# Reciprocal-root chains moved between engines, two small weight vectors stored once, and a mixing step issued later, in a two-block model kernel

## The chip, the cores and the metric

The kernel runs on one core of one Trainium2 chip. The metric is device microseconds of one execution of the whole program; the time before is the median of 3 runs, 1548.84 us (1548.0 to 1549.24).

## The reference, cut to what matters

Two blocks over x of shape (1, 256, 1024), all in float32. Block 1 is a gated spatial unit, a causal attention with forget gates and a SwiGLU layer; block 2 is a mixer of pooling, mLSTM and attention with normalised heads, a cross attention, and 16 experts that each take 32 tokens.

```python
def rmsnorm(x, g):
    r = lax.rsqrt(jnp.mean(xf * xf, axis=-1, keepdims=True) + EPS)
    return xf * r * g
def spatial_gating(u, v, w_s, b_s, g_v):            # chunks of 128 tokens
    v = layernorm(v, g_v)
    mixed = einsum('gts,bcsgd->bctgd', tril(w_s), vc) + b_s
    return u * mixed
def first_block(x, ...):
    h = rmsnorm(x, mix_pre_g); proj = h @ w_in      # u, v_s, q, k, v_a, g_a, g_b, f
    merged = sigmoid(g_a) * spatial_gating(gelu(u), gelu(v_s), ...) + sigmoid(g_b) * attention
    x = x + rmsnorm(merged @ w_out, mix_post_g)
    x = x + rmsnorm(swiglu(rmsnorm(x, ffn_pre_g), w_gate, w_up, w_down), ffn_post_g)
def head_rmsnorm(a, g):                             # 8 query and 2 key heads of 64, one g of 64 for each kind
    return a * lax.rsqrt(mean(a * a, -1) + EPS) * g
def second_block(x, mem, ...):
    x = x + concat[pool, mlstm, attn(head_rmsnorm(q), head_rmsnorm(k))] @ w_out
    x = x + mem_cross_attn(rmsnorm_2(x), mem, ...)
    x = x + ec_moe(rmsnorm_2(x), router_w, w_gu, w_down)   # 16 experts, 24 MB of weights each
    return rmsnorm_2(x, final_norm_g)
```

## The kernel before, in words

The 256 tokens stand as two tiles t of 128 partitions. Weights come from memory through one queue, SyncE's (SP in the profile), in pieces of 1 MB into three buffers named raw. `split` (L57 to L70) turns each piece into a high part, written by ScalarE (L67, two halves), and a low part, written by VectorE (L68, two halves of 1.2 us each), in four buffers named whl. A matmul of float32 precision is then three matmuls on the parts (`mm3`, L86). Activations are split in the same way after they have been transposed: ScalarE writes xh (L118), VectorE writes xl (L119).

A normalisation of a token tile runs over four engines: ScalarE sums squares (L151), VectorE adds two halves (L153), a chain of nine tiny instructions on a 128x1 column makes 1/sqrt (`rstd`, L121 to L139: three to prepare, then three Newton steps of two), VectorE scales the tile (L172 for `scale`, L209 for `post_norm_c`, L332 in the layer norm), TensorE transposes it (L185). Chains of width 1 go to GpSimd (POOL) unless the caller names VectorE; wider ones are on VectorE. Nine chains run on GpSimd: tile 1 of the first norm, both tiles of the layer norm of v, four at the end of block 1's mixing (post norm and next norm, tiles 0 and 1), and two at the end of the SwiGLU layer (tile 1).

Each engine executes its instructions in one fixed order, which a planner sets at compile time with its own estimates of durations; the program's order counts as priority. `issue_after` (in `queued`, with the lists `self.behind`) adds edges by hand, so that certain weight splits stand behind certain norm steps or ahead of them: at the end of block 1's mixing, for example, `post_norm_c` of tile 1 stands behind the low part of a split, and the next `scale` too.

Block 1's mixing projects v (two pieces of 512 columns, `vs`), normalises it, then projects u in four pieces (`proj_W`, g = 0, 2, 4, 6), and multiplies each with the spatial mixing of v (`mixed(g)`, L341: 8 matmuls, then two VectorE operations). Before, `mixed(g - 2)` comes right after projection g. The SwiGLU layer runs over 11 slices j of 256 hidden columns: gate and up of slice j, then the down product of slice j - 1 (`aH`, `aL` are its activations, L546 to L550).

Block 2's small tables are loaded by DMAs in `block2_mix`, which the planner issues early, between the weights of the SwiGLU layer. `g640` holds the head norms' weights spread to 10 heads of 64 in each partition; its first 8 heads are scaled by 0.125 (L665) and the whole is multiplied into q and k (L917).

The experts (`moe`, from L1063) stream 402 MB through 12 slots of 2 MB, eight loads of w_gu and four of w_down an expert (L1083); several slots lie where earlier stages had their buffers. TensorE works on a slot as it lands.

Of the kernel before, what the change touches and what calls it, by code (L numbers as in the profile page):

```python
# [14 lines left out]
OP = mybir.AluOpType  # L15
# [4 lines left out]
D = 1024  # L20
# [6 lines left out]
class Body:  # L27
# [90 lines left out]
        self.nc.scalar.activation(H, src, AF.Copy)  # L118
        self.at["E"] = self.nc.vector.tensor_tensor(L, src, H.bitcast(F32), OP.subtract).ins  # L119

    def rstd(self, ss, n, scale, tag="rs", eng=None):  # L121

        nc = self.nc
        q = self.small.tile([128, 4, n], F32, name="rstd", tag=tag + str(n), bufs=4 if n == 1 else 2)
        v, h, y, t = (q[:, i, :n] for i in range(4))
        e = eng or (nc.gpsimd if n == 1 else nc.vector)
        e.tensor_scalar(v, ss, scale, EPS, OP.mult, OP.add)
        e.tensor_scalar(y.bitcast(I32), v.bitcast(I32), -0.5, float(0x5F3759DF), OP.mult, OP.add)
        e.tensor_scalar(h, v, -0.5, None, OP.mult)
        for _ in range(3):  # L130
            if n == 1:
                e.tensor_scalar(t, y, y, h, OP.mult, OP.mult)
                self.last = e.tensor_scalar(y, t, 1.5, y, OP.add, OP.mult)
            else:
                nc.vector.tensor_tensor(t, y, y, OP.mult)
                nc.vector.tensor_tensor(t, t, h, OP.mult)
                nc.vector.scalar_tensor_tensor(y, t, 1.5, y, OP.add, OP.mult)
        return y
# [18 lines left out]
    def norm_T(self, x, gname):  # L157

        nc = self.nc
        g = self.gain(gname)  # L160
        H = self.sb(self.xt, [128, 8, 256], "xh", F32R, tag="xh")
        L = self.sb(self.xt, [128, 8, 256], "xl", F32R, tag="xl")

        def factor(t, eng=None):
            h = self.work.tile([128, D], F32, name="hn", tag="work")
            r = self.rstd(self.sumsq([x[:, t, 0:512], x[:, t, 512:D]], h), 1, 1.0 / D, eng=eng)
            self.at["s", t] = self.sq
            return h, r

        def scale(t, h, r):  # L170
            for c in (slice(0, 512), slice(512, D)):
                self.at["h", t] = nc.vector.scalar_tensor_tensor(h[:, c], x[:, t, c], r, g[:, c], OP.mult, OP.mult).ins  # L172
            return h

        def trans(t, h):
            self.trans_HL(H, L, h, t)

        return (H, L), factor, scale, trans
# [7 lines left out]
            self.evac_HL(H[:, 4 * q:4 * q + 4, t * 128:(t + 1) * 128], L[:, 4 * q:4 * q + 4, t * 128:(t + 1) * 128],  # L186
                         p.rearrange("p (k c) -> p k c", k=4))

    def post_norm_a(self, t, halves, eng=None):

        junk = self.work.tile([128, D], F32, name="pj", tag="work")
        ss = self.sumsq(halves, junk)
        self.at["q", t] = self.sq
        return self.rstd(ss, 1, 1.0 / D, "rsp", eng)

    def post_norm_b(self, halves, g):

# [15 lines left out]
    def run(self):  # L213
        tc, nc, a, ctx = self.tc, self.nc, self.a, self.ctx
        self.per = self.open("per", 1)
        self.small = self.open("small", 4)
        self.banks = None
        self.behind, self.at = [], {}
        self.psum_pool(acc=4, sm=4)
        self.xtp = ExitStack()  # L220
        self.xt = self.open("xt", 1, self.xtp, "right")
        self.NR, self.NH = 3, 4
        self.ep = self.open("ep", 1)
        self.big = self.open("big", 1)
        rawst = ExitStack()
        self.rawp = self.open("rawp", 1, rawst)
        st = ExitStack()
        self.work = self.open("work", 3, st)
        self.gains = self.open("gains", 2, st)
        per = self.per  # L230
        x = self.x = self.sb(per, [128, 2, D], "x")
        xr = a["x"][0].rearrange("(t p) d -> p t d", p=128)
        nc.sync.dma_start(x[:, 0, :], xr[:, 0, :])
        xT, factor, scale, trans = self.norm_T(self.x, "mix_pre_g")
        nc.sync.dma_start(x[:, 1, :], xr[:, 1, :])
        first = [self.unit(a["w_in"][0], u, 1024) for u in range(2)]
        self.constants()
        mkv = ExitStack()
        self.mkv = self.open("mkv", 1, mkv, "right")
        memp = ExitStack()  # L240
        self.memp = self.open("memp", 1, memp, "right")
        for t in range(2):
            trans(t, scale(t, *factor(t, None if t else nc.vector)))
        xT, wg = self.block1_mix(xT, first)
        xT = self.block1_ffn(xT, wg)
        xT = self.block2_mix(*xT, memp, st)
        self.cross(xT)
        self.close(rawst, mkv, self.xtp)
        self.moe()
        self.psum_st.close()  # L250
# [38 lines left out]
    def block1_mix(self, xT, first):  # L289
        tc, nc, a = self.tc, self.nc, self.a  # L290
        w_in = a["w_in"][0]
        with ExitStack() as es:
# [21 lines left out]
            for q in range(2):  # L314
                p = self.ps()
# [34 lines left out]
            for g in (0, 2, 4, 6):  # L350
                acc = self.proj_W(xT, w_in, 128 * g)
                nc.scalar.activation(pair(z, g), bank(acc), AF.Gelu_apprx_tanh)
                if g:
                    mixed(g - 2)
            mixed(6)

            wfH = self.sb(m1, [128, 8, 8], "wfH", F32R)
# [175 lines left out]
    def block1_ffn(self, xT, wg0):  # L533
# [4 lines left out]
        with ExitStack() as es:  # L538
# [42 lines left out]
                    down(j, acts[j], ds[j], (t,))  # L581

            tail(0)
            r = self.post_norm_a(0, acc[0:2], nc.vector)
            self.post_norm_c(0, self.post_norm_b(acc[0:2], gp), r)
            h = scale(0, *factor(0, nc.vector))
            tail(1)
            r = self.post_norm_a(1, acc[2:4])
            p = self.at
# [31 lines left out]
    def block2_mix(self, xT, wk, wq, trans1, memp, st):  # L621
        tc, nc, a = self.tc, self.nc, self.a
        wi = a["w_in_2"][0]
        with ExitStack() as es:
# [8 lines left out]
            nc.sync.dma_start(cw, a["mlstm_conv_w_2"][0].rearrange("j (b p) -> (j b) p", p=128))  # L633
            mng = self.sb(m2, [128, 256], "mng")
            nc.sync.dma_start(mng, bcast(a["mlstm_norm_g_2"][0]))
            g640 = self.sb(m2, [128, 10, 64], "g640")
            for h0, n, nm in ((0, 8, "q_norm_g_2"), (8, 2, "k_norm_g_2")):
                g1 = a[nm][0]
                nc.sync.dma_start(g640[:, h0:h0 + n, :],
                                    bass.AP(tensor=g1.tensor, offset=g1.offset, ap=[[0, 128], [0, n], [1, 64]]))  # L640
            rope = self.sb(m2, [128, 2, 2, 64], "rope")
            nc.sync.dma_start(rope, a["rope_c"])
            pw = self.sb(m2, [128, 2, 128], "pw")
# [18 lines left out]
                nc.scalar.activation(qa[:, t, 0:8, :], acc.rearrange("p (h e) -> p h e", h=8), AF.Copy)  # L662
            self.close(st)
            nc.vector.tensor_scalar(mng, mng, 0.5, None, OP.mult)
            nc.vector.tensor_scalar(g640[:, 0:8, :], g640[:, 0:8, :], 0.125, None, OP.mult)  # L665
            ms = ExitStack()
            mw = self.open("m2w", 2, ms, "right")
            wg = mw.tile([128, 8, 16], F32, name="wg", tag="pd", bufs=1)
            nc.sync.dma_start(wg, wi.rearrange("(k p) c -> p k c", p=128)[:, :, 1280:1296])
            wqk = [self.split(self.unit_c(wi, 256 + 128 * b)) for b in (0, 2)]  # L670
            self.psum_pool(acc=2, at=3, po=1, sm=2)
            qT, kT = self.attn2_rope(m2, qa, g640, rope)

            wgH = self.sb(m2, [128, 8, 16], "wgH", F32R)
            wgL = self.sb(m2, [128, 8, 16], "wgL", F32R)
# [37 lines left out]
            self.work = self.open("work2", 2, work2)  # L713
            self.gains = self.open("gains2", 1, work2)
            xT, factor, scale, trans = self.norm_T(self.x, "norm_mem_g_2")
            self.proj_out(a["w_out_2"][0], (yH, yL), lambda t: trans(t, scale(t, *factor(t, nc.vector))), ((2, 3, 0, 1), (4, 5, 6, 7)), ("acc", "sm"))
            p = self.at
            self.behind = [(), (p["h", 0], p["s", 0])]
            self.close(work2)
# [182 lines left out]
                nc.tensor.transpose(py[:, b * 256 + t * 128:b * 256 + t * 128 + 128], hf[:, b * 128:(b + 1) * 128], self.ident)  # L902
        self.evac_HL(yH[:, 2:4, :], yL[:, 2:4, :], py.rearrange("p (b t) -> p b t", b=2))

    def attn2_rope(self, m2, qa, g640, rope):
        nc = self.nc
        qT = self.sb(m2, [128, 4, 256], "qT2")
        kT = self.sb(m2, [128, 256], "kT2")
# [3 lines left out]
        ss = self.small.tile([128, 32], F32, name="ss", tag="st6", bufs=1)  # L912
        nc.vector.tensor_reduce(ss[:, 0:20].rearrange("p (t h) -> p t h", t=2), ro, AX.X, OP.add)
        r = self.rstd(ss[:, 0:20], 20, 1.0 / 64)
        qa2, g2 = qa.rearrange("p t h e -> p (t h) e"), g640[:, None].to_broadcast([128, 2, 10, 64])
        nc.vector.tensor_tensor(qa2, qa2, r[:, :, None].to_broadcast([128, 20, 64]), OP.mult)
        nc.vector.tensor_tensor(qa, qa, g2, OP.mult)  # L917
        for t in range(2):
            av2 = qa[:, t].rearrange("p h (f two) -> p h f two", two=2)
            rv = ro[:, t].rearrange("p h (f two) -> p h f two", two=2)  # L920
# [117 lines left out]
    def route(self, t, cw):  # L1038
# [4 lines left out]
        for q in range(2):  # L1043
# [6 lines left out]
                nc.vector.tensor_copy(xf[:, 0:4], p)  # L1050
            else:
                nc.scalar.activation(xf[:, 4:8], p, AF.Copy)
        self.r4[t] = self.rstd(ss, 1, 1.0 / D, eng=nc.vector)
        self.r4_ins[t] = self.last.ins
        nc.gpsimd.tensor_copy(self.rc[:, t:t + 1], self.r4[t])
        p = self.logits[t] = self.ps("po" if t else "at")
# [242 lines left out]
```

## Time and profile before

| | |
|---|---|
| median of 3 runs | 1548.84 us (1548.0 to 1549.24) |
| the profiled execution, its own time | 1550.03 us |
| its span on the core | 1548.3 us |
| mean granted TensorE clock | 0.884 |
| TensorE busy | 1202.1 us (78%) |
| VectorE / ScalarE / GpSimd busy | 421.3 / 352.3 / 37.4 us |
| read from memory | 501 MB |

The span is cut in two by what is busy: up to about 575 us TensorE is busy nearly all the time, afterwards the DMA engines are. A time of the trace is us from the start of the span. In a timeline row the bracket at the end says how long the engine was idle before the instruction and what ended that idle time.

### The profile page before, as it was taken

The page shows a single profiled execution, that of the slowest core. Times are in us where ns is not written, and L with a number is a line of the kernel's source. Part 1 is how long each engine was busy: PE and PEld are TensorE (multiplying, and loading weights), DVE is VectorE, ACT ScalarE, POOL GpSimd, SP SyncE. Part 2 cuts the span into 40 slices and gives each one's busy share as a digit, 9 for nine tenths or more (in the row PEclk, how much of TensorE's full clock was granted, in tenths as well). Part 3 has the DMA queues.
Part 4 walks back from the last instruction along what each step waited for, and adds up shares of the span by engine and source line. Part 5 has one row for each costly group of instructions (what it writes and reads, how often), then busy time and mean ns, then how long its engine had stood idle before and what let it go on. Part 6 is the DMA issues. An engine that isn't in the chain of part 4 may idle for free.

```text
span 1548.3 us, 17883 instructions
## 1 busy us (share of the span) xinstructions
PE 1202.1 (78%) x7685; PEld 684.1 (44%) x7685; DVE 421.3 (27%) x769; ACT 352.3 (23%) x608; POOL 37.4 (2%) x97
## 2 busy tenths in 40 slices
PE   6999998999989999786666666657666566567675
PEld 5998988899978786321112111112111112111112
DVE  5644655545466765300000000000000000000002
ACT  5455544444445744010000000000000000000002
POOL 1100012000020000000000000000000000000000
PEclk9999999999999999898769878788788788877777
DMA  8754444755543349999999999999999999999996
GB/s 284 227 165 143 138 136 152 257 182 189 190 124 124 110 176 407 369 428 427 427 428 427 426 428 428 427 428 426 428 427 427 427 427 427 428 428 426 427 425 233
DMA packets 110127, 503.26 MB, mean 325 GB/s; under 512 B 11083, under 2 KB 65119, under 8 KB 85984
## 3 DMA queue, kind: packets, MB, share of 16 engines
q1 hardware_dynamic: 110048, 502.12, 81.5%
q8 instruction: 60, 0.98, 0.3%
q14 instruction: 19, 0.16, 0.0%
HBM read 501.05 MB, written 1.05 MB: 324 GB/s over the span
## 4 chain that ended last, share of the span: by engine, by line
DMA 54%; PE 2%; SPq 2%; DVE 1%; ACT 0%; issue 0%; DVEq 0%
DMA eraw<-in_expert_w_gu_dram 36%; DMA eraw<-in_expert_w_down_dram 18%; SPq L1233 2%; PE sm L1153 1%; PE sm L1186 1%; PE sm L1135 0%; PE acc L1200 0%; DVE tk L1108 0%; DVE m L1107 0%; DVE OH L1119 0%; ACT L1173 0%; DVE x L1242 0%; PE sm L1177 0%; DVE ys L1198 0%; DVE es L1174 0%
## 5 line engine op out<-in xcount | busy, mean ns | idle before, releaser
L1153 PE MATMUL sm<-eraw,xs 128*32 128x512 f32 x2048 | 330.5, 755 | 190.2 <-DMA eraw<-in_expert_w_gu_dram 190.2
L1153 PEld LDWEIGHTS sm<-eraw,xs 128*32 128x32 f32 x2048 | 63.3, 124 | 429.7 <-DMA eraw<-in_expert_w_gu_dram 289.5
L1186 PE MATMUL sm<-eraw,aT 128*32 128x512 f32 (+2 forms) x1088 | 169.1, 758 | 81.6 <-DMA eraw<-in_expert_w_down_dram 73.4
L68 DVE TENSOR_TENSOR whl<-raw,whl 128x1024 fp32r<-128x1024 f32 x166 | 198.0, 1220 | 107.7 <-ACT whl L67 107.6
L67 ACT ACTIVATE whl<-raw 128x1024 fp32r<-128x1024 f32 x166 | 168.2, 1052 | 91.5 <-issue 49.7
L1174 DVE SCALAR_TENSOR_TENSOR es<-sm,rsl,es 128x512 f32<-128x512 f32 x16 | 12.0, 751 | 465.7 <-PE sm L1153 462.8
L1186 PEld LDWEIGHTS sm<-eraw,aT 128*32 128x32 f32 x1088 | 34.6, 129 | 198.7 <-DMA eraw<-in_expert_w_down_dram 118.3
L1173 ACT ACTIVATE es<-sm,rsl 128x512 f32<-128x512 f32 x16 | 11.0, 687 | 427.2 <-PE sm L1153 427.2
L86 PE MATMUL acc<-xh,whl 128*128 128x256 f32 x704 | 95.8, 286 | 0.0
L86 PE MATMUL sm<-xh,whl 128*128 128x256 f32 x704 | 91.7, 283 | 0.0
L86 PEld LDWEIGHTS acc<-xh,whl 128*128 128x128 f32 x704 | 88.8, 191 | 0.8
L86 PEld LDWEIGHTS sm<-xh,whl 128*128 128x128 f32 x704 | 88.2, 191 | 0.6
L1198 DVE COPY ys<-sm 128x512 f32<-128x512 f32 (+2 forms) x18 | 11.4, 631 | 235.9 <-PE acc L1200 231.4
L86 PE MATMUL acc<-whl,xh 128*128 128x512 f32 x256 | 70.5, 408 | 0.2
L1200 PE MATMUL acc<-ys,ogT 128*128 128x512 f32 (+2 forms) x136 | 66.3, 611 | 5.2 <-DVE ys L1198 4.3
L1196 ACT ACTIVATE ys<-sm 128x512 f32<-128x512 f32 x16 | 9.6, 597 | 229.9 <-PE sm L1186 229.9
L86 PE MATMUL acc<-whl,aH 128*128 128x512 f32 x176 | 57.9, 403 | 2.4 <-ACT aH L118 2.4
L86 PEld LDWEIGHTS acc<-whl,xh 128*128 128x128 f32 x256 | 48.1, 192 | 11.6 <-ACT xh L118 0.6
L86 PE MATMUL acc<-xl,whl 128*128 128x256 f32 x352 | 51.0, 283 | 0.0
L86 PE MATMUL sm<-xl,whl 128*128 128x256 f32 x352 | 48.9, 281 | 0.0
L1200 PEld LDWEIGHTS acc<-ys,ogT 128*128 128x128 f32 x136 | 23.9, 199 | 51.5 <-issue 21.4
L86 PEld LDWEIGHTS acc<-xl,whl 128*128 128x128 f32 x352 | 45.5, 189 | 0.4
(366 smaller groups left out, 1124.0 us busy)
## 6 DMA issues: line engine op xcount, KB each, us to landing
eraw<-in_expert_w_gu_dram SPq DMA_DIRECT2D x128, 2048.0 KB, 39.1
eraw<-in_expert_w_down_dram SPq DMA_DIRECT2D x60, 2048.0 KB, 39.1
raw<-in_w_in_dram SPq DMA_DIRECT2D x34, 1024.0 KB, 5.4
raw<-in_w_gate_dram SPq DMA_DIRECT2D x11, 1024.0 KB, 5.3
raw<-in_w_up_dram SPq DMA_DIRECT2D x11, 1024.0 KB, 5.5
raw<-in_w_down_dram SPq DMA_DIRECT2D x11, 1024.0 KB, 5.0
raw<-in_w_out_dram SPq DMA_DIRECT2D x8, 1024.0 KB, 5.6
eraw<-in_expert_w_down_dram SPq DMA_DIRECT2D x7, 1024.0 KB, 27.8
```

The source lines that it names most:

```text
L67: nc.scalar.activation(H[:, k], raw[:, k], AF.Copy)
L68: self.at["L"] = nc.vector.tensor_tensor(L[:, k], raw[:, k], H[:, k].bitcast(F32), OP.subtract).ins
L86: nc.tensor.matmul(out, l[i], r[j], start=first and p == 0 and q == 0, stop=last and p == 2 and q == n - 1)
L1153: nc.tensor.matmul(dst[32 * j:32 * j + 32, :], xs[:, k, 32 * q:32 * q + 32], raw[:, o + 512 * j:o + 512 * j + 512], start=k == 0, stop=k = ...
L1173: nc.scalar.activation(s, G, AF.Silu, scale=rs)
L1174: nc.vector.scalar_tensor_tensor(s, U, rs, s, OP.mult, OP.mult)
L1186: nc.tensor.matmul(y[c0][32 * c:32 * c + 32, 0:n], aT[:, c, 32 * j:32 * j + 32], raw[:, o:o + n], start=j == 0, stop=j == 3, tile_position ...
L1196: nc.scalar.activation(ys, y[c0][:, 0:n], AF.Copy)
L1198: nc.vector.tensor_copy(ys, y[c0][:, 0:n])
L1200: nc.tensor.matmul(out[t], ogT[:, t * 128:(t + 1) * 128], ys, start=first, stop=last)
L1233: nc.sync.dma_start(raws[j].rearrange("p (i n) -> p i n", i=4)[:, :, c0:c0 + m], rows(j)[:, :, c0:c0 + m])
```

## The change

All chains of `rstd` go to VectorE, whatever their width; the parameter `eng` goes. The two head norms' weights are loaded once per partition, as `gqk` of 128 x 2 x 64, and multiplied in by two VectorE operations with a broadcast operand, one over the 8 query heads and one over the 2 key heads, in place of one over 10. `mixed(g)` comes two projections after projection g, in place of one; the last two come after the last projection.

```diff
-    def rstd(self, ss, n, scale, tag="rs", eng=None):
+    def rstd(self, ss, n, scale, tag="rs"):
...
-        e = eng or (nc.gpsimd if n == 1 else nc.vector)
+        e = nc.vector
...
             for g in (0, 2, 4, 6):
                 acc = self.proj_W(xT, w_in, 128 * g)
                 nc.scalar.activation(pair(z, g), bank(acc), AF.Gelu_apprx_tanh)
-                if g:
-                    mixed(g - 2)
+                if g >= 4:
+                    mixed(g - 4)
+            mixed(4)
             mixed(6)
...
-            g640 = self.sb(m2, [128, 10, 64], "g640")
-            for h0, n, nm in ((0, 8, "q_norm_g_2"), (8, 2, "k_norm_g_2")):
-                g1 = a[nm][0]
-                nc.sync.dma_start(g640[:, h0:h0 + n, :],
-                                    bass.AP(tensor=g1.tensor, offset=g1.offset, ap=[[0, 128], [0, n], [1, 64]]))
+            gqk = self.sb(m2, [128, 2, 64], "gqk")
+            for i, nm in enumerate(("q_norm_g_2", "k_norm_g_2")):
+                nc.sync.dma_start(gqk[:, i, :], bcast(a[nm][0]))
...
-            nc.vector.tensor_scalar(g640[:, 0:8, :], g640[:, 0:8, :], 0.125, None, OP.mult)
+            nc.vector.tensor_scalar(gqk[:, 0, :], gqk[:, 0, :], 0.125, None, OP.mult)
...
-        nc.vector.tensor_tensor(qa, qa, g2, OP.mult)
+        for i, hh in enumerate((slice(0, 8), slice(8, 10))):
+            nc.vector.tensor_tensor(qa[:, :, hh], qa[:, :, hh],
+                                    gqk[:, None, i:i + 1, :].to_broadcast([128, 2, hh.stop - hh.start, 64]), OP.mult)
```

The other lines of the diff drop the argument `eng` from `factor`, `post_norm_a` and their callers.

## Rows read from the trace of the kernel before

**Rows 1.** The page's part 2, 40 slices of the span: busy tenths of the DMA engines.

```profile
DMA  8754444755543349999999999999999999999996
```

**Rows 2.** The chain of work that ended last: start us, us, what.

```profile
673.90 30.19 DMA eraw<-in_expert_w_down_dram
```

**Rows 3.** Timeline of SyncE's queue: start us, us, line, out<-in, count.

```profile
573.58 27.72 SPq L1083 DMA_DIRECT2D eraw<-in_expert_w_gu_dram  x8
```

**Rows 4.** Timeline of a chain of nine on VectorE: its first instruction and its successor.

```profile
441.55 0.15 DVE L127 TENSOR_SCALAR rstd<-ss 128x1 f32<-128x1 f32 x1
443.67 1.42 DVE L172 SCALAR_TENSOR_TENSOR hn<-x,rstd,gain 128x512 f32<-128x512 f32 x2
```

**Rows 5.** Timeline around the first spatial mixing, TensorE and VectorE.

```profile
42.76 2.04 PE L86 MATMUL acc<-xh,whl 128*128 128x256 f32 x16
50.86 0.81 DVE L332 TENSOR_SCALAR vs<-vs,mv,rstd 128x1024 f32<-128x1024 f32 x1 [3.07 <-POOL rstd L133]
53.99 0.94 PE L341 MATMUL sm<-wb,vs 128*128 128x128 f32 x6 [2.41 <-DVE vs L333]
54.69 3.61 PE L86 MATMUL acc<-xh,whl 128*128 128x256 f32 x16
```

**Rows 6.** Timeline of SyncE's queue and VectorE around the load of the query norm's weights.

```profile
254.04 0.43 SPq L639 DMA_DIRECT2D g<-in_q_norm_g_dram  x1
258.53 9.66 SPq L56 DMA_DIRECT2D raw<-in_w_up_dram  x1
272.41 0.43 DVE L665 TENSOR_SCALAR g<-g 128x512 f32<-128x512 f32 x1 [13.70 <-DMA g<-in_q_norm_g_dram]
275.49 1.06 ACT L67 ACTIVATE whl<-raw 128x1024 fp32r<-128x1024 f32 x1 [15.23 <-DMA raw<-in_w_gate_dram]
```

**Rows 7.** Windows: stretch, us, busy of PE PEld DVE ACT POOL, PEclk, DMA share, GB/s.

```profile
260.00:262.00 2.00, 2.00 (x19) 2.00 (x19) 0.00 (x0) 0.25 (x1) 0.00 (x0) 1.00 0.07 20
274.70:286.17 11.47, 8.51 (x24) 6.46 (x25) 9.80 (x11) 7.65 (x9) 0.00 (x0) 0.70 0.91 287
297.56:303.20 5.64, 5.64 (x28) 4.67 (x27) 3.65 (x4) 2.53 (x3) 0.00 (x0) 1.00 0.65 191
```

**Rows 8.** DMA issues: out<-in, queue, count, KB each, median us to landing.

```profile
mng<-in_mlstm_norm_g_dram SPq DMA_DIRECT2D x1, 128.0 KB, 4.7
g<-in_k_norm_g_dram SPq DMA_DIRECT2D x1, 64.0 KB, 6.7
```

**Rows 9.** Timeline at the end of block 1's mixing, VectorE and ScalarE, then TensorE.

```profile
233.88 1.42 DVE L172 SCALAR_TENSOR_TENSOR hn<-x,rstd,gain 128x512 f32<-128x512 f32 x2 [2.15 <-POOL rstd L133]
241.06 1.41 DVE L209 SCALAR_TENSOR_TENSOR x<-pn,rstd,x 128x512 f32<-128x512 f32 x2 [2.23 <-POOL rstd L133]
243.60 1.22 DVE L68 TENSOR_TENSOR whl<-raw,whl 128x1024 fp32r<-128x1024 f32 x1
244.72 3.90 ACT L67 ACTIVATE whl<-raw 128x1024 fp32r<-128x1024 f32 x4
247.88 1.41 DVE L172 SCALAR_TENSOR_TENSOR hn<-x,rstd,gain 128x512 f32<-128x512 f32 x2 [3.06 <-POOL rstd L133]
...
248.78 0.63 PE L185 MATMUL sm<-ident,hn 128*128 128x128 f32 x4 [3.46 <-DVE hn L172]
```

**Rows 10.** VectorE's busy time in a stretch at the end of the SwiGLU layer.

```profile
443.00:448.00 5.00, 4.89 (x11) 1.00 0.00 0
```

**Rows 11.** Timeline behind that stretch, VectorE and TensorE.

```profile
450.35 1.42 DVE L209 SCALAR_TENSOR_TENSOR x<-pn,rstd,x 128x512 f32<-128x512 f32 x2 [0.53 <-POOL rstd L133]
459.43 1.41 DVE L172 SCALAR_TENSOR_TENSOR hn<-x,rstd,gain 128x512 f32<-128x512 f32 x2 [3.06 <-POOL rstd L133]
460.33 1.71 PE L185 MATMUL sm<-ident,hn 128*128 128x128 f32 x8 [2.64 <-DVE hn L172]
```

**Rows 12.** Timeline of VectorE at the start, and in the head norm.

```profile
13.51 1.42 DVE L172 SCALAR_TENSOR_TENSOR hn<-x,rstd,gain 128x512 f32<-128x512 f32 x2 [2.23 <-POOL rstd L133]
...
481.77 1.49 DVE L917 TENSOR_TENSOR qa<-qa,g 128x1280 f32<-128x1280 f32 x1
```

More of the change, by code (lines that the diff above doesn't have):

```diff
@@ L162, in norm_T, with factor @@
         L = self.sb(self.xt, [128, 8, 256], "xl", F32R, tag="xl")
-        def factor(t, eng=None):
+        def factor(t):
             h = self.work.tile([128, D], F32, name="hn", tag="work")
-            r = self.rstd(self.sumsq([x[:, t, 0:512], x[:, t, 512:D]], h), 1, 1.0 / D, eng=eng)
+            r = self.rstd(self.sumsq([x[:, t, 0:512], x[:, t, 512:D]], h), 1, 1.0 / D)
             self.at["s", t] = self.sq
@@ L187, in trans_HL, with post_norm_a @@
                          p.rearrange("p (k c) -> p k c", k=4))
-    def post_norm_a(self, t, halves, eng=None):
+    def post_norm_a(self, t, halves):
         junk = self.work.tile([128, D], F32, name="pj", tag="work")
@@ L193, in post_norm_a @@
         self.at["q", t] = self.sq
-        return self.rstd(ss, 1, 1.0 / D, "rsp", eng)
+        return self.rstd(ss, 1, 1.0 / D, "rsp")
     def post_norm_b(self, halves, g):
@@ L242, in run @@
         for t in range(2):
-            trans(t, scale(t, *factor(t, None if t else nc.vector)))
+            trans(t, scale(t, *factor(t)))
         xT, wg = self.block1_mix(xT, first)
@@ L583, in block1_ffn @@
             tail(0)
-            r = self.post_norm_a(0, acc[0:2], nc.vector)
+            r = self.post_norm_a(0, acc[0:2])
             self.post_norm_c(0, self.post_norm_b(acc[0:2], gp), r)
-            h = scale(0, *factor(0, nc.vector))
+            h = scale(0, *factor(0))
             tail(1)
@@ L671, in block2_mix @@
             self.psum_pool(acc=2, at=3, po=1, sm=2)
-            qT, kT = self.attn2_rope(m2, qa, g640, rope)
+            qT, kT = self.attn2_rope(m2, qa, gqk, rope)
             wgH = self.sb(m2, [128, 8, 16], "wgH", F32R)
@@ L715, in block2_mix @@
             xT, factor, scale, trans = self.norm_T(self.x, "norm_mem_g_2")
-            self.proj_out(a["w_out_2"][0], (yH, yL), lambda t: trans(t, scale(t, *factor(t, nc.vector))), ((2, 3, 0, 1), (4, 5, 6, 7)), ("acc", "sm"))
+            self.proj_out(a["w_out_2"][0], (yH, yL), lambda t: trans(t, scale(t, *factor(t))), ((2, 3, 0, 1), (4, 5, 6, 7)), ("acc", "sm"))
             p = self.at
@@ L903, in mlstm, with attn2_rope @@
         self.evac_HL(yH[:, 2:4, :], yL[:, 2:4, :], py.rearrange("p (b t) -> p b t", b=2))
-    def attn2_rope(self, m2, qa, g640, rope):
+    def attn2_rope(self, m2, qa, gqk, rope):
         nc = self.nc
@@ L914, in attn2_rope @@
         r = self.rstd(ss[:, 0:20], 20, 1.0 / 64)
-        qa2, g2 = qa.rearrange("p t h e -> p (t h) e"), g640[:, None].to_broadcast([128, 2, 10, 64])
+        qa2 = qa.rearrange("p t h e -> p (t h) e")
         nc.vector.tensor_tensor(qa2, qa2, r[:, :, None].to_broadcast([128, 20, 64]), OP.mult)
-        nc.vector.tensor_tensor(qa, qa, g2, OP.mult)
+        for i, hh in enumerate((slice(0, 8), slice(8, 10))):
+            nc.vector.tensor_tensor(qa[:, :, hh], qa[:, :, hh],
+                                    gqk[:, None, i:i + 1, :].to_broadcast([128, 2, hh.stop - hh.start, 64]), OP.mult)
         for t in range(2):
@@ L1052, in route @@
                 nc.scalar.activation(xf[:, 4:8], p, AF.Copy)
-        self.r4[t] = self.rstd(ss, 1, 1.0 / D, eng=nc.vector)
+        self.r4[t] = self.rstd(ss, 1, 1.0 / D)
         self.r4_ins[t] = self.last.ins
```

## The prediction

> **What bounds the kernel now.** First the page's slices: the DMA engines are full from the 16th of 40 slices to the end [rows 1]. Then the chain of waits, read from its end: between 673.90 us and the last loads it holds nearly nothing but loads of expert weights, the first of them in [rows 2]; compute after them and a few hundredths of issue are all the rest. So the end is set by when that stream begins and by its bytes, which the change leaves alone. SyncE's timeline shows the beginning: the first expert load is issued at 573.58 us, into buffers that the stages before have to give up [rows 3]. Up to there TensorE is busy nearly all the time, so I read its timeline for every idle stretch and every slow one ahead of 573 us. What is taken out of these comes off the stream's start and, one for one, off the end; VectorE, ScalarE or GpSimd time as such is worth nothing. Four places matter, and all have a part of the change at their root.
>
> **The price of a chain.** On VectorE the nine instructions run from 441.55 to 443.67, 2.12 us [rows 4]. Nine chains move: 9 x 2.12 = 19.1 us more VectorE work. While a chain runs on GpSimd, VectorE mostly stands idle until it ends, so each move is a difference: 2.12 us of work for an idle time that stands in a bracket.
>
> **Place A, spatial mixing (54 us).** The first mixing's last six matmuls stand 2.41 us idle, waiting for VectorE's gain on v, which itself waited 3.07 us for a GpSimd chain [rows 5]. The idle stretch has a second price: the next 16 projection matmuls take 3.61 us, where the same 16 took 2.04 before, a clock lower for 1.57 us. Now the third projection comes first. It is 48 matmuls at 2.04/16, 6.1 us; put in at about 51.6 (2.41 ahead of 53.99) it has TensorE busy until about 57.5, while the operands are there at 53.99 even with the chains left on GpSimd, and some us earlier with 2.12 in place of 3.07 for each tile. The cover is 3.5 us thick. The mixing's own matmuls are moved, not added; its VectorE steps lie later, but z is not read before the gates, far behind. On SyncE, loads that wait for v's gain go sooner. Sum: -2.41 - 1.57 = -4.0 us; if the cover failed, 0.
>
> **Place B, the query norm's weights (254 to 286 us).** The load issued at 254.04 has 128 x 8 rows of 256 bytes. Everything behind it suffers: SyncE's next-but-one issue takes 9.66 us, VectorE stands 13.70 us in front of its scaling at 272.41 with work behind it in the line, ScalarE waits 15.23 us for a gate weight [rows 6]. Six us after the issue the 16 DMA engines are 0.07 busy and move 20 GB/s [rows 7]: one engine's share, for 256 KB at that rate 13 us. At last TensorE pays: the down product's 24 matmuls of slice 0 fill 11.47 us at clock 0.70; the next slice's take 5.64 with a few more besides [rows 7]. That is 5.83 us of waiting and clock. The new load has 128 rows. Not in the trace, but between 1.6 us (32 KB at 20 GB/s) and the 6.7 that 256 rows took, near the 4.7 of another load of 128 rows [rows 8]; I take 4.7. Landed by 259 to 261, it leaves VectorE over 10 us before the first activation of the layer needs it, so even the upper end costs nothing. -5.8 us; bounds -6.0 and, should the queue stay blocked for another reason, 0. The key weights' second load shrinks too; nobody waits for it.
>
> **Place C, end of block 1's mixing (245 us).** TensorE waits 3.46 us for the scaled tile 1 [rows 9]. Its line goes back through three GpSimd waits. (1) VectorE idles 2.15 us before 233.88 for tile 0's chain; that chain, sooner and shorter, frees VectorE when tile 1's sums arrive: about 1.9 us. (2) The 2.23 us before 241.06 turn into 2.12 us of chain, with the split ahead of it as now: 0.1. (3) From 243.60 to 247.88 there are 4.28 us: half a split, 1.22, and 3.06 of waiting. On VectorE it is 2.12 if the half split goes behind, 3.34 if it stays ahead: 0.9 to 2.2. The tile is 2.9 to 4.2 us sooner. What is late next: ScalarE's four split halves, 3.90 us at 244.72, stand ahead of the evacuation of these very transposes; they move up with ScalarE's sums, by about 2 to 2.5 us. I take -3.2, between the two; bounds -5.0 (ScalarE reordered, some clock back) and -2.0.
>
> **Place D, end of the SwiGLU layer (445 to 460 us).** Here the move costs. VectorE is 4.89 of 5 us busy [rows 10], with splits that the next tile's scaling stands behind by an edge. It waits for GpSimd only 0.53 us before 450.35 and 3.06 before 459.43 [rows 11]. In exchange come two chains: 2 x 2.12 - 0.53 - 3.06 = +0.65 for the scaled tile 1 that TensorE waits for at 460.33. The first chain also precedes tile 0's low part, up to 2.12 for TensorE some us earlier; but TensorE loses 2.64 idle us at 460.33 anyway, and a stall ahead of that is taken out of it. I take +0.6; bounds -0.7 (the shorter last wait leaves the clock up: the eight transposes took 1.71 us at a lower one) and +4.2 (both chains in the open).
> A page speaks against the move exactly here: the Trainium skill, Perfetto Trace Analysis, section "Optimizing Scalar/DVE Operations", says that from a saturated VectorE work may be moved off, even to GpSimd. By it D would cost up to the 4.2; by the rows 0.65, because VectorE was idle waiting for the engine that relieved it. The same section doubts that shifting between these two helps, since they share a port; the 3.06 us wait behind splits agrees in direction.
>
> **Small parts.** At the start VectorE idles 2.23 us for tile 1's chain [rows 12] and would work 2.12 instead: 0; bounds -0.5 and +2.1 (chain put ahead of tile 0's scaling). The product with the norm weights, 1.49 us for 1280 elements [rows 12], becomes one of 1024 and one of 256: the same elements and one more fixed part, +0.1; bounds 0 and +0.4, TensorE having gate projections meanwhile. The scaling by 0.125 shrinks eightfold, in a place where VectorE has room.
>
> **Sum.** -4.0 - 3.2 + 0.6 - 5.8 + 0.1 = -12.3 us. The profiled execution took 1550.03, so 1537.7; the median of the runs is 1.2 lower, so 1536.5. Bounds summed naively: -4.0 - 5.0 - 0.7 - 6.0 - 0.5 = -16.2, so 1532.6; if the planner also reorders block 2 by a us or two in my favour, 1531.
>
> **Rivals.** *VectorE gives part of it back.* At C and D the chains run into splits, D costs 4.2 and C yields 2.0: -4.0 - 2.0 + 4.2 - 5.8 + 0.1 = -7.5, so 1541.3. For it: [rows 10] and the splits' edges. Against it: the brackets, which show that VectorE was idle for the same time. The page's rule named at D would give this outcome, 1541.3. In the same band lies B failing (1542.3): if many reads of one 256-byte row were slow by themselves rather than by their number; the key weights' 256 rows in 6.7 us speak against that.
> *All goes together.* C yields 5.0 and D gains 0.7: -4.0 - 5.0 - 0.7 - 5.8 + 0.1 = -15.4, so 1533.4, and down to 1531 with the other lower bounds.
> *The gain is hidden.* The stream does not start sooner, because something other than TensorE's line gives up its buffers: within 3 us of before, 1548. Against it: the queue's loads ahead of that one belong to stages that TensorE paces, and its slots lie where those stages work.
> *Slower: an in-order VectorE.* Every chain instruction stands in one line with the splits and low parts that TensorE eats. If the planner lays the chains' first instructions, which wait for ScalarE's sums, ahead of ready splits, chains end up on TensorE's line in full: 2.12 each, and where TensorE then stands over 2 us, some 1.6 of clock as in [rows 5], 3.7 together. The moves of mixing and weights bring 4.0 + 5.8 = 9.8, so from the third such chain on nothing is left, and six (all but the layer norm's two and the first) cost 22: 1548.8 - 9.8 + 22 = 1561. Against it: the chain that already stands between a ready tile and TensorE ran unbroken [rows 4].
>
> **Chances.** The forecast (1533.5 to 1540.5) 0.60; part given back, or B failing (1540.5 to 1545.5) 0.16; all together (below 1533.5) 0.10; hidden 0.06; slower 0.08. No change is what lies within 0.2%, 3.1 us, about what a measurement can tell. So faster 0.86, same 0.06, slower 0.08. For the range I keep the forecast, half of "all together" and most of the given-back band up to 1543.5: 1531.5 to 1543.5, about 0.8.
>
> **What would show it.** GpSimd has no 128x1 arithmetic left. A: no TensorE wait for v, the clock whole at 55 to 60. B: no VectorE wait for the query weights above 2 us, the first down product near 5.6 us. C: the wait of 3.46 below 1.5. D: tile 1's transposes 0 to 1 us later against the layer's end than before. The first expert load near 561, and from it to the end the same 975 us within 2. The prediction is wrong if that load moves by less than 8 us, if a new TensorE wait for a VectorE split appears, or if the stretch from the load to the end grows.

## Result and the profile after

The changed kernel takes 1537.2 us (median of 4 runs, 1536.8 to 1539.4), beside 1549.04 for the kernel before on the same chip (4 runs, 1548.0 to 1550.9): ratio 0.9928, 95% interval 0.9912 to 0.9943. The forecast was 1536.5, in a range from 1531.5 to 1543.5. The profiled execution has a span of 1535.2 us, 13.1 less than before; the first expert load is issued 12.58 us sooner, and from it to the end there are 974.2 us (974.7 before). As forecast, the end moved with the start of that stream and, but for 0.5 us, with nothing else; in the traces of all fourteen kernels here that stretch is 973.3 to 975.5 us. On the page GpSimd is down to 5.0 us in 16 instructions and VectorE up to 434.3 from 421.3.

The four places, first on TensorE's timeline (start us, us, engine, line, operation, out<-in, shapes, count, and in brackets the idle time before and what ended it). Line numbers of this kernel differ from the one before by at most one.

```profile
10.77 1.94 PE L185 MATMUL sm<-ident,hn 128*128 128x128 f32 x8 [10.77 <-DVE hn L172]
12.54 2.17 PE L86 MATMUL acc<-whl,xh 128*128 128x512 f32 x4
...
55.19 1.05 PE L341 MATMUL sm<-wb,vs 128*128 128x128 f32 x8
56.00 2.15 PE L86 MATMUL acc<-xh,whl 128*128 128x256 f32 x16
...
243.40 1.93 PE L185 MATMUL sm<-ident,hn 128*128 128x128 f32 x8 [3.88 <-DVE hn L172]
246.09 3.99 PE L86 MATMUL sm<-xh,whl 128*128 128x256 f32 x17 [0.75 <-ACT xh L118]
...
444.81 1.67 PE L86 MATMUL acc<-whl,xh 128*128 128x512 f32 x6 [0.48 <-DVE rstd L127]
...
449.70 1.29 PE L185 MATMUL sm<-ident,hn 128*128 128x128 f32 x8 [1.35 <-DVE hn L172]
```

At 55.19 the wait of 2.41 us of [rows 5] is gone and the clock is whole. At 243.40 the wait of [rows 9] is not shorter but longer, 3.88 for 3.46, with slow matmuls behind it. At 449.70 tile 1's wait of 2.64 [rows 11] is 1.35. The wait of 0.48 at 444.81 is new: it ends 0.06 us after a split half of VectorE (443.53 to 444.75), with the chain instruction behind that half named as what ended it. A new wait for a split is what the prediction had named as a sign of being wrong; here it is small. Of the prediction's other signs, C's (the wait of 3.46 below 1.5) failed.

Now the query norm's weights and the stream, on SyncE's queue, and two windows, the first gate product and the first down product (us, busy of PE, PEld, DVE, ACT, POOL, PEclk, DMA share, GB/s):

```profile
245.62 0.42 SPq L639 DMA_DIRECT2D gqk<-in_q_norm_g_dram  x1
...
251.44 0.38 SPq L56 DMA_DIRECT2D raw<-in_w_up_dram  x1
...
561.00 28.32 SPq L1084 DMA_DIRECT2D eraw<-in_expert_w_gu_dram  x8
```

```profile
246.00:250.00 4.00, 3.91 (x18) 3.91 (x19) 4.00 (x5) 2.76 (x4) 0.00 (x0) 0.50 0.62 208
...
270.58:276.07 5.49, 5.49 (x26) 4.51 (x25) 3.65 (x4) 2.53 (x3) 0.00 (x0) 1.00 0.65 190
```

The issue that took 9.66 us [rows 6] takes 0.38, and the down product that took 11.47 [rows 7] takes 5.49. The gate product behind the longer wait runs at a granted clock of 0.50, the lower of the two levels, 1.2 GHz.

To keep books I use the lead: how much sooner than in the kernel before TensorE starts the same instruction. What the lead gains between two points was gained there. The points are the first u-projection (39.94 us before), the forget gate's first matmul (70.23), the memory keys' second projection (239.37), gate projection 1 (263.14), tile 0's transposes at the end of the SwiGLU layer (444.57), block 2's gate weights (474.23) and the first expert load (573.58). "Start" is the lead at the first point; A is what was gained from the first to the second, C from the third to the fourth, B from the fourth to the fifth, D from the fifth to the sixth. One profiled execution each, us; the last row is the changed kernel's forecast:

| kernel | start | A | C | B | D | lead at load | time, ratio to before |
|---|---|---|---|---|---|---|---|
| changed | 1.65 | 4.20 | -1.97 | 6.38 | 1.72 | 12.58 | 1537.2, 0.9928 |
| mixing alone | -0.13 | 4.09 | -0.50 | 0.30 | -0.27 | 3.45 | 1545.0, 0.9983 |
| weights alone | -0.80 | 1.66 | 0.05 | 6.18 | 0.90 | 8.21 | 1541.6, 0.9965 |
| chains alone | 1.51 | 3.68 | -2.02 | 6.27 | 1.72 | 11.38 | 1538.0, 0.9944 |
| forecast | 0 | 4.0 | 3.2 | 5.8 | -0.6 | 12.3 | 1536.5 |

### The profile page after: what moved, and what is told of

It is laid out like the page before. It is cut to its first block, busy times and chain, and to the rows that moved or that the text cites. A ratio compares the mean times of both kernels' runs of the same rounds, so it can differ in the third digit from the quotient of the medians.

```text
span 1535.2 us, 17874 instructions
## 1 busy us (share of the span) xinstructions
PE 1190.9 (78%) x7685; PEld 677.8 (44%) x7685; DVE 434.3 (28%) x851; ACT 351.7 (23%) x608; POOL 5.0 (0%) x16
## 4 chain that ended last, share of the span: by engine, by line
DMA 54%; PE 2%; SPq 2%; DVE 1%; issue 0%; ACT 0%; DVEq 0%
DMA eraw<-in_expert_w_gu_dram 36%; DMA eraw<-in_expert_w_down_dram 18%; SPq L1234 2%; PE sm L1154 1%; PE sm L1187 1%; PE sm L1136 0%; DVE tk L1109 0%; DVE m L1108 0%; PE acc L1201 0%; DVE OH L1120 0%; DVE x L1243 0%; ACT L1174 0%; PE sm L1178 0%; DVE es L1175 0%; DVE eraw L1251 0%
## 5 line engine op out<-in xcount | busy, mean ns | idle before, releaser
L1154 PE MATMUL sm<-eraw,xs 128*32 128x512 f32 x2048 | 324.3, 742 | 190.2 <-DMA eraw<-in_expert_w_gu_dram 190.2
L68 DVE TENSOR_TENSOR whl<-raw,whl 128x1024 fp32r<-128x1024 f32 x166 | 198.8, 1221 | 116.9 <-ACT whl L67 116.7
```

The lines of the kernel that those rows point to most:

```text
L68: self.at["L"] = nc.vector.tensor_tensor(L[:, k], raw[:, k], H[:, k].bitcast(F32), OP.subtract).ins
L1154: nc.tensor.matmul(dst[32 * j:32 * j + 32, :], xs[:, k, 32 * q:32 * q + 32], raw[:, o + 512 * j:o + 512 * j + 512], start=k == 0, stop=k = ...
```

## Experiments

Times of the runs below are medians, each set against the kernel before on the same chip (1547.5 to 1548.6 there); brackets hold the 95% interval of the ratio to it.

**1 to 3. Each part alone.** Edits: the hunks of the diff for the mixing, for the weights, and for the chains (in the third, one line):

```
-        e = eng or (nc.gpsimd if n == 1 else nc.vector)
+        e = nc.vector
```

> The kernel before with one edit: each spatial mixing stands two projections later; chains and head-norm weights as before. Theory (the parts add up, each acts at its own place): TensorE's wait of 2.41 us for v and the clock lost behind it go, 4.0 to 4.2 us; first expert load near 569.5, time 1544.6 to 1545.2. Rival (the gain at A in the changed kernel needed the layer norm's chains on VectorE too): with v only ready at 53.99 less wait is saved, 2 us or under, 1547. Rival (given back at a later place, as the loads that follow come no sooner): under 1 us, 1548 to 1549.

> The kernel before with one edit: the two head norms' weights are loaded once per partition and spread over the heads in the product; chains and mixing as before. Theory: the slow down product of slice 0 (11.47 us) takes 5.5, lead +6.0 at the start of gate projection 2, and +0.0 at the start of gate projection 1; time 1542.6 to 1543.2. Rival for the loss at the end of block 1's mixing (the load queue's new order costs it, not the chains): gate projection 1 starts 1.5 to 2 us later than its lead before that place, time 1544.5 to 1545.

> The kernel before with one edit: all nine-instruction chains on VectorE; mixing and weights as before. Theory (the chains gain where VectorE idled for them and lose where split halves stand between their instructions): start -1.6, spatial mixing 0 (TensorE still stands some 2.5 us in front of the first mixing), end of block 1's mixing +2.0, end of the SwiGLU layer -1.8, block 2 -0.6: 1546.5 to 1547.5. Forecast's own terms (0, none of A, -3.2, +0.6, 0): 1546.4, but with the end of block 1's mixing 3.2 shorter. Rival (chains cost nothing anywhere, the loss at block 1's mixing comes from the load queue): 1544.5 to 1545.

Measured: mixing 1545.0 (ratio 0.9973 to 0.9992), weights 1541.6 (0.9952 to 0.9977), chains 1538.0 (0.9927 to 0.9961). The first came out as expected, the second 1.0 below its range. The third was a miss by 8.5 us or more, and it overturns the picture of separate places: 2.9 + 6.3 + 9.9 = 19.1 us for the parts, some 12 for the whole. The table shows where: the chains alone bring A's 3.7 and B's 6.3 too, with the mixing where it was and the slow load as it was. At A, the operands of the first mixing come so soon, and the order puts twelve of a projection's 48 matmuls in front:

```profile
49.97 1.65 PE L86 MATMUL acc<-xh,whl 128*128 128x256 f32 x12
51.74 0.93 PE L341 MATMUL sm<-wb,vs 128*128 128x128 f32 x6
```

The run of the weights alone says something else of A. It has the wait of [rows 5] (2.34), yet the 16 matmuls behind it take 2.12 us, not 3.61:

```profile
54.73 0.94 PE L341 MATMUL sm<-wb,vs 128*128 128x128 f32 x6 [2.34 <-DVE vs L333]
55.42 2.12 PE L86 MATMUL acc<-xh,whl 128*128 128x256 f32 x16
```

**4 and 5. Is B hidden by the chains, and by which?** Run 4 is the changed kernel with the weights' hunk undone. Run 5 is chains alone with the four chains of block 1's end left on GpSimd (`post_norm_a(t, acc, nc.gpsimd)` and `factor(t, nc.gpsimd)` in `block1_mix`).

> The changed kernel without its weights edit: chains on VectorE and the later mixing, but the query norm's weights loaded as before, 128 x 8 rows. Theory after the chains alone gave 9.9 us (the parts overlap: with the chains on VectorE the slow load is issued 8 us sooner and lands before TensorE needs what stands behind it): first down product near 5.5 us long, no TensorE wait in front of it, 1536.6 to 1538.0, within 0.7 of the changed kernel. Rival (the forecast's sum, each part at its own place): the 5.8 us come back, 1542 to 1543.5.

> The kernel before with the chains on VectorE except the four at the end of block 1's mixing, which stay on GpSimd; mixing and weights as before. Theory (the gate split's low halves that stand between that chain's instructions free a raw buffer early, SyncE's queue goes on, and the query norm's slow load is issued 8 us sooner; so the loss at block 1's mixing and the hidden load have one cause): without them w_down's first slice and the slow load are issued about as late against TensorE as before, TensorE waits 1.5 to 3 us in front of the first down product and runs it at a lower clock, and 3 to 6 of the 9.9 us are lost: 1541 to 1544. Rival (the chains hide the slow load in some other way): no wait there, and the 1.2 us lost at block 1's mixing are gained, 1536 to 1537.

Measured: 1538.3 (0.9921 to 0.9946; B 6.43) and 1541.9 (0.9950 to 0.9977; C +0.15, B 0.92). Run 5 is as the theory had it, run 4 too, 0.3 above its range. With the chains on VectorE the small load is worth nothing that can be measured; with block 1's four chains back on GpSimd the price returns. SyncE's queue, chains alone first, then run 5:

```profile
241.88 0.37 SPq L556 DMA_DIRECT2D raw<-in_w_down_dram  x1
...
245.99 0.42 SPq L639 DMA_DIRECT2D g<-in_q_norm_g_dram  x1
250.67 0.38 SPq L56 DMA_DIRECT2D raw<-in_w_gate_dram  x1
```

```profile
247.74 0.38 SPq L556 DMA_DIRECT2D raw<-in_w_down_dram  x1
...
249.00 0.43 SPq L639 DMA_DIRECT2D g<-in_q_norm_g_dram  x1
251.21 0.38 SPq L56 DMA_DIRECT2D raw<-in_w_gate_dram  x1
```

Down's first slice waits for a raw buffer. Where a gate unit's low halves run early (next experiment), it is free 5.9 us sooner, and the slow load 3.0 sooner, with TensorE only 0.3 further on. ScalarE still stands 11.25 us for the gate unit behind it, until 268.11, but TensorE comes to the down product at 271.13, without a wait (chains alone, ScalarE and TensorE):

```profile
268.11 1.06 ACT L67 ACTIVATE whl<-raw 128x1024 fp32r<-128x1024 f32 x1 [11.25 <-DMA raw<-in_w_gate_dram]
271.13 0.39 PE L86 MATMUL acc<-whl,aH 128*128 128x512 f32 x1
```

**6. What costs C?** VectorE, and one row of ScalarE, in the changed kernel:

```profile
236.15 0.16 DVE L153 TENSOR_TENSOR ss<-ss 128x1 f32<-128x1 f32 x1
236.22 1.22 DVE L68 TENSOR_TENSOR whl<-raw,whl 128x1024 fp32r<-128x1024 f32 x1
237.36 0.15 DVE L127 TENSOR_SCALAR rstd<-ss 128x1 f32<-128x1 f32 x1
237.42 1.21 DVE L68 TENSOR_TENSOR whl<-raw,whl 128x1024 fp32r<-128x1024 f32 x1
...
239.00 1.22 DVE L68 TENSOR_TENSOR whl<-raw,whl 128x1024 fp32r<-128x1024 f32 x1
240.14 0.21 DVE L133 TENSOR_SCALAR rstd<-rstd 128x1 f32<-128x1 f32 x1
240.26 1.22 DVE L68 TENSOR_TENSOR whl<-raw,whl 128x1024 fp32r<-128x1024 f32 x1
...
242.50 1.42 DVE L172 SCALAR_TENSOR_TENSOR hn<-x,rstd,gain 128x512 f32<-128x512 f32 x2
```

```profile
244.50 1.06 ACT L67 ACTIVATE whl<-raw 128x1024 fp32r<-128x1024 f32 x1 [4.11 <-DMA raw<-in_w_up_dram]
```

The order puts four halves of weight splits in, one between the addition of the sums (L153) and the chain, three inside the chain: addition and chain, 2.31 us without a break (run 7), take from 236.15 to 242.50. Run 6 puts these four chains back on GpSimd in the changed kernel (the edit of run 5).

> The changed kernel with one edit: the four chains at the end of block 1's mixing are on GpSimd as before; everything else as changed. Theory (the 2.0 us lost there come from split halves standing between the chain's instructions on VectorE, which makes 2.12 us of chain last 6.1): the lead over the kernel before, 5.8 at the memory keys' second projection, is 5.8 again at gate projection 1 instead of 3.8, so 2.0 off the changed kernel's 1537.2: 1535.0 to 1535.6. Rival (the gate weights' loads set that place, since ScalarE stands 4.11 us for w_up's first slice ahead of the evacuation): the lead stays 3.8 and the time 1537.

Measured: 1536.05 (0.9916 to 0.9945), C -0.19 for -1.97. The place answers as expected; the total is 0.45 above the expected range and does not separate from the changed kernel's.

**7 and 8. The chain unbroken, with the small load and with the slow one.** Edges make the split halves follow the chain (`queued` orders an instruction behind the named ones of its engine):

```
+        self.at["EA"] = self.nc.scalar.activation(H, src, AF.Copy).ins
...
-            self.behind = [(p["x", 1], p["q", 1])]
+            self.behind = [(p["h", 1], p["q", 1])]
...
-            self.behind = [(p["E"], p["s", 1])]
+            self.behind = [(p["E"], p["s", 1]), (p["E"],), (p["E"], p["EA"])]
```

> The changed kernel with four order edges at the end of block 1's mixing: the low halves of the first gate unit's split stand behind tile 1's scaling on VectorE, those of the next gate unit behind tile 1's low parts, and the next up unit's behind these and, on ScalarE, behind the evacuation of tile 1's transposes. Nothing stands between the chain's instructions then. Theory (broken chain and ScalarE's 4.11 us in front of a weight slice cost the place): chain about 2.1 us, TensorE's wait of 3.88 falls below 1, the 17 gate matmuls take 2.1 to 3.2 instead of 3.99; lead at gate projection 1 from 3.8 to 7 to 8.5; time 1532.5 to 1534.5 where the changed kernel has 1537.2. Rival (the raw buffers come free later, so the next units land later and TensorE waits for them instead): 1536.5 or more, with a new wait for a split.

> The changed kernel with the four order edges of the version that ran at 1530.35, but with the query norm's weights loaded as before, 128 x 8 rows. Theory (the weights edit is worth what the order leaves of the slow load's price): the slow load is issued near 248.6 and lands near 267, TensorE reaches the first down product near 264 and waits 3 us or more for it, then runs at a lower clock: 1535 to 1538, 5 to 7 more than with the small load, although the same edit was worth under 1 in the changed kernel. Rival (the order edges hide the load as the broken chain did): 1530 to 1531.5.

Measured: 1530.35 (0.9870 to 0.9897) and 1530.88 (0.9872 to 0.9905). The first is the fastest kernel here, 6.9 below the changed one (ratio 0.9884 for 0.9928), and beat its expectation: C +4.92, B 6.29, lead at the load 19.16. VectorE, then TensorE, in run 7:

```profile
236.37 0.16 DVE L153 TENSOR_TENSOR ss<-ss 128x1 f32<-128x1 f32 x1
...
238.68 1.42 DVE L172 SCALAR_TENSOR_TENSOR hn<-x,rstd,gain 128x512 f32<-128x512 f32 x2
240.01 2.35 DVE L68 TENSOR_TENSOR whl<-raw,whl 128x1024 fp32r<-128x1024 f32 x2
```

```profile
239.59 1.28 PE L185 MATMUL sm<-ident,hn 128*128 128x128 f32 x8
241.15 2.29 PE L86 MATMUL sm<-xh,whl 128*128 128x256 f32 x17 [0.28 <-ACT xh L118]
```

Addition and chain take 2.3 us, TensorE does not wait for the scaled tile, and the 17 matmuls take 2.29 for 3.99. The split that stood ahead of ScalarE's evacuation is out of the way as well, here as in run 6, so what each of the two cost by itself is not shown. Run 8 went against my theory: B is 6.30 with the slow load too. Its queue and ScalarE show why:

```profile
248.30 0.38 SPq L56 DMA_DIRECT2D raw<-in_w_gate_dram  x1
248.73 0.58 SPq L640 DMA_DIRECT2D g<-in_q_norm_g_dram  x1
252.67 1.33 SPq L56 DMA_DIRECT2D raw<-in_w_up_dram  x1
```

```profile
256.67 1.06 ACT L67 ACTIVATE whl<-raw 128x1024 fp32r<-128x1024 f32 x1 [2.48 <-DMA raw<-in_w_gate_dram]
257.63 0.62 ACT L118 ACTIVATE aH<-si 128x512 fp32r<-128x512 f32 x1
...
270.54 2.01 ACT L67 ACTIVATE whl<-raw 128x1024 fp32r<-128x1024 f32 x2 [10.85 <-DMA raw<-in_w_up_dram]
```

Here the gate unit is issued ahead of the slow load and is there 8.4 us later; the up unit behind it takes 17.9, but the first activation's evacuation (aH) stands ahead of it in ScalarE's line.

**9 and 10. What is the price of the slow load?** Run 9 fetches the same rows by ten loads, run 10 takes VectorE's wait of 13.70 us off the line and leaves the load:

```
+                for h1 in range(h0, h0 + n):
+                    nc.sync.dma_start(g640[:, h1, :], bcast(g1))
```

```
+            with self.queued([self.at["E"]]):
                 nc.vector.tensor_scalar(g640[:, 0:8, :], g640[:, 0:8, :], 0.125, None, OP.mult)
```

> The kernel before with one edit: the same 1280 rows of 256 bytes of head-norm weights are fetched by ten loads of 128 rows instead of one of 1024 and one of 256. Theory (the form of the one load, with its inner stride of 0, is slow): each lands within 4 to 7 us of its issue, VectorE waits under 3 us for them, and the 6 us come as with the smaller load, less up to 1 for eight more issues of 0.43 us on SyncE's queue: 1541.5 to 1543. Rival (the number of reads of one row sets the pace, 20 GB/s in all): the last of the eight lands 13 us or more after the first is issued, and the time is 1546 to 1549.

> The kernel before with one edge: the scaling of the query norm's weights by 0.125, in front of which VectorE stood 13.70 us with the splits and the first activation's product behind it, is ordered behind the last low part of the next layer's transposes, some 190 us later; the load itself stays as it is, 128 x 8 rows. Theory, after the last run (what TensorE pays is the gate unit issued 2 us behind the slow load, which lands only when the slow load is done, some 19 us after its issue, and in front of whose split ScalarE stands with the evacuation for the first down product behind it): VectorE's wait is gone, but ScalarE's 15.23 us for the gate weight, TensorE's 2.42 us and the slow down product stay: 1547 to 1549. Rival (the forecast's wording: VectorE's wait holds up the down product): the first down product takes near 5.5 us without a wait, 1541.5 to 1543.

Measured: 1542.8 (0.9955 to 0.9979; B 6.29) and 1547.96 (0.9987 to 1.0013; B -0.05). So one load of 1024 rows holds up what is behind it, and eight of 128 rows, spread among the weights' loads, do not: the gate unit behind the first of them lands 6.2 us after its issue, for 19.1 before. Two expected numbers were missed: the eight loads land in 8.0 us (median; I had expected 4 to 7), and VectorE stands 6.65 us for the key norm's, though TensorE does not pay for it. Whether the load's form makes it slow or only the number of rows in one load stays open, since what the rival expected came too: the last of the eight lands more than 13 us after the first is issued (254.34; the last is issued near 270). The Trainium skill, DMA: Bandwidth & Descriptors, section "Why a DMA increments its semaphore by 16 and not by 1", would have a load of 128 partitions split over 16 engines; the share of 0.07 in [rows 7] for the one with an inner stride of 0, about one engine's worth of 16, does not agree, and the measurement decides (no row shows which engines worked). Run 10 names the payer. VectorE is free early, and TensorE waits as before, for ScalarE, which stands in front of the gate unit issued 2.2 us behind the slow load:

```profile
263.23 0.69 DVE L547 TENSOR_TENSOR si<-si,sm 128x512 f32<-128x512 f32 x1 [1.57 <-PE sm L86]
```

```profile
275.59 1.06 ACT L67 ACTIVATE whl<-raw 128x1024 fp32r<-128x1024 f32 x1 [15.38 <-DMA raw<-in_w_gate_dram]
276.56 0.61 ACT L118 ACTIVATE aH<-si 128x512 fp32r<-128x512 f32 x1
```

```profile
277.22 0.80 PE L86 MATMUL acc<-whl,aH 128*128 128x512 f32 x1 [2.76 <-ACT aH L118]
```

**11 and 12. D and the start.** The changed kernel with one move undone each: tile 1's two chains at the layer's end on GpSimd (`post_norm_a(1, acc[2:4], nc.gpsimd)`, `factor(1, nc.gpsimd)`), and tile 1's chain at the start (`factor(t, nc.gpsimd if t else None)`).

> The changed kernel with the two chains of tile 1 at the end of the SwiGLU layer on GpSimd as before. Theory (the chains on VectorE gained 1.8 us there, against a forecast of 0.6 lost, since low halves run between their instructions while TensorE has other work): TensorE's wait for the scaled tile 1 goes from 1.35 back to 2.6, its eight transposes from 1.29 to 1.7, the lead over the kernel before falls by 1.5 to 2 between the transposes of tile 0 and block 2's gate weights: 1538.5 to 1539.5. Rival (the forecast's term): 0.6 faster than the changed kernel, 1536.6, its lead rising there.

> The changed kernel with the chain of tile 1 at the start on GpSimd as before. Theory (1.65 us of lead at the first u-projection came from this chain, which the forecast put at 0): TensorE waits 1.6 us for the scaled tile 1 near 14.3, the lead at the first u-projection falls to about 0, and nothing behind it takes that back: 1538.6 to 1539.2. Rival (the lead at the start came from the loads of x and the first weights, which differ between executions by as much: 0.80 later in one kernel whose start was not touched): lead above 1, 1536.5 to 1537.6.

Measured: 1540.4 (0.9935 to 0.9960), 0.9 above its range, and 1539.0 (0.9928 to 0.9951). D falls from 1.72 to -0.35, the start from 1.65 to -0.20. The waits are back:

```profile
451.54 1.29 PE L185 MATMUL sm<-ident,hn 128*128 128x128 f32 x8 [2.64 <-DVE hn L172]
```

```profile
14.49 1.97 PE L185 MATMUL sm<-ident,hn 128*128 128x128 f32 x8 [1.61 <-DVE hn L172]
```

## Why the prediction was right, and where it was not

Terms are written as in the prediction, where minus is time saved. The bound was right: the expert stream's start sets the end. The total was right partly by luck, because errors cancelled: C came out 5.2 worse than its term, and the start (1.65), D (2.3), B (0.6) and A (0.2) together 4.7 better; the rest is in block 2.

*A* (-4.0; -4.20). Right in size against the one trace of before, and the mixing alone does it, but so do the chains, which the working priced at nothing there: "the operands are there at 53.99 even with the chains left on GpSimd" asked only whether the move suffices, not whether it is needed. The second price, 1.57 us of clock, was that of one execution: in runs 2, 9 and 10, whose A was untouched, A gained 1.7 to 1.8 by itself (with starts 0.8 to 1.5 later). In the medians the mixing alone is worth 2.9.

*B* (-5.8; -6.38). Right in size; the payer was named among the sufferers [rows 6], but VectorE's 13.70 us were not part of it (run 10), and its bounds, "-6.0 and, should the queue stay blocked for another reason, 0", treated it as independent of the chains. It is a matter of order on the queue: the price falls due if the unit behind the slow load is still out when TensorE comes to what stands behind it in ScalarE's line. Issued 2.2 us behind a late load it is due in full or nearly (before and run 10; run 5, where 0.92 of it is gained); behind a load 3.0 us sooner (chains alone), or with that unit ahead of the load (run 8), there is none.

*C* (-3.2, bounds -5.0 and -2.0; measured +1.97). This step failed: "On VectorE it is 2.12 if the half split goes behind, 3.34 if it stays ahead". A chain is nine instructions, each placed by itself, and together with the addition ahead of it, it was broken open by four halves; of [rows 4], the row that carried the price, I had made a fixed block. Up to the addition of tile 1's sums there is a gain, as (1) and (2) had it: VectorE comes to it 7.38 us sooner (236.15 for 243.53), where TensorE's lead is 5.8. Step (3) lost 2.0 us where 0.9 to 2.2 were to be gained: from there to the scaling it was 4.35 us and is 6.35. On top of it ScalarE's next split, waiting 4.11 us for its unit, stood ahead of the evacuation. Of the 1.97 us, TensorE's longer wait is only 0.4; 0.75 go on the transposes and their evacuation, and 0.8 on the 17 gate matmuls, 3.99 us at the lower clock against these before:

```profile
250.72 3.21 PE L86 MATMUL sm<-xh,whl 128*128 128x256 f32 x17
```

Unbroken, the place gives 4.92, nearly the lower bound. The rival with "C yields 2.0" foresaw a smaller gain, not a loss. And C's loss and B's cover have a common root: the halves that broke the chain freed the raw buffer.

*D* (+0.6, bounds -0.7 and +4.2; measured -1.72, by run 11 -2.07). "In exchange come two chains" summed them as if in one block; the order laid low halves and splits between them while TensorE had other products, and two GpSimd waits went. So tile 1's transposes start 0.43 us sooner after tile 0's (15.33 us for 15.76), not 0.65 later. The same freedom that cost C paid here. The other 1.29 us are the clock, which the working had only in a bound. Two windows, before and changed, from tile 1's transposes to the same matmul behind them (columns as above):

```profile
460.33:464.90 4.57, 4.53 (x16) 3.65 (x17) 2.10 (x4) 1.39 (x3) 0.00 (x0) 0.63 0.10 38
449.70:452.98 3.28, 3.22 (x17) 2.42 (x18) 2.07 (x4) 1.39 (x3) 0.00 (x0) 1.00 0.60 174
```

The clock is 0.63 and 1.00. In the five other traces with these two chains on GpSimd the wait is 2.64 to 2.66 us and D lies between -1.58 and 0.90, as the clock behind the wait falls; in all eight with them on VectorE it is 1.72 or 1.73. Of what the Trainium skill, Perfetto Trace Analysis, section "Optimizing Scalar/DVE Operations", says, the advice to take work off a saturated VectorE, even to GpSimd, was no guide here: from 432 to 450 us VectorE of the changed kernel is busy 17.47 of 18 us, and taking the two chains off it (run 11) cost 2.07 us of lead. Its doubt that shifting work between these two helps agrees.

*The start* (0, bounds -0.5 and +2.1; -1.65). It set VectorE's idle 2.23 against 2.12 of work and did not ask what TensorE does meanwhile: at 12.54 it now has projection products, and tile 1's transposes follow later. The start differs between executions, but not by enough to explain it: -1.53 to -0.13 in the five other traces with that chain on GpSimd, 0.99 to 1.51 in the seven others with it on VectorE. *Head norm* (+0.1) is within 0.1.

Rivals: no gain was hidden, and the in-order VectorE decided at C alone. What stays open: by which costs the written order came to put the halves into the chain, what the broken chain and ScalarE's split each cost at C, and whether the changed kernel beats chains alone, since their intervals overlap.

## What to carry to other kernels

Gains that hang on the same wait do not add: before summing the parts of a change, ask for each stall whether another part already removes it. A chain of tiny instructions moved to a shared in-order engine costs what the order puts between them, so price it with the ready work around it, and give it edges if TensorE waits for its end. A slow load's price is that of the unit queued behind it and of what stands behind that unit's first reader.

## What the hardware showed

The same wait of 2.3 to 2.4 us on TensorE was followed in one execution by 3.61 us for 16 matmuls at a mean granted clock of 0.53, near the lower of its two levels of 1.2 and 2.4 GHz, in another by 2.12 us at the whole clock. In the same way eight transposes behind a wait of 2.64 to 2.66 us took 1.29 to 1.94 us in six traces. So a price of clock that one execution shows is not yet that of the kernel.

GpSimd's chain did not run beside VectorE's split halves (L68) and scalings (L172). Of its 81 chain instructions in the kernel before, 71 take 0.19 to 0.34 us, nine of these inside a VectorE instruction that reads acc or sm (L119, L201). The other ten take 0.67 to 3.37; each starts inside a split half or a scaling and ends within 0.21 us of the end of one (spans on GpSimd are rough). The longest, GpSimd and then VectorE, before:

```profile
453.06 3.37 POOL L127 TENSOR_SCALAR rstd<-ss 128x1 f32<-128x1 f32 x1 [2.74 <-DVE ss L153]
456.51 0.19 POOL L128 TENSOR_SCALAR rstd<-rstd 128x1 int32<-128x1 int32 x1
```

```profile
452.89 3.49 DVE L68 TENSOR_TENSOR whl<-raw,whl 128x1024 fp32r<-128x1024 f32 x3
```

So these chains did not use the time of the splits, and VectorE waited for them afterwards, 3.06 us here [rows 11].

And a load of 1 MB issued 2.2 us behind the slow 256 KB one landed 19 us after its issue (256.37 to 275.59), where such loads take 5.3 (the page's median for gate weights).
